# A hybrid attention block: priority of weight parts and of the differential heads' norms, a shared tile, and one more temporary

## The chip, the cores and the metric

The kernel runs on one core of a Trainium2 chip. The metric is the time of one execution on the device in microseconds; of several executions the median counts. A profile comes from one further execution, whose own time is named beside its span.

## The reference

One decoder block over 512 tokens of width 1024, in float32. Two attention branches share one input projection; a gated sum of both, an output projection, a residual and a feed-forward part follow.

```python
xn = rmsnorm(x, norm_mix_g)
proj = xn @ w_in          # q_lat, kv_lat, k_rope, dq, dk, dv, gate_pre
# branch A: 8 heads of latent attention, 64 + 32 rotated columns each
q = rmsnorm(q_lat) @ w_uq;  kv = rmsnorm(kv_lat) @ w_ukv
o_mla = causal_attention(cat(q_nope, rope(q_pe)), cat(k_nope, rope(k_rope)), v)
# branch B: 4 differential heads, each of two softmaxes over 64 columns
o_diff = rmsnorm(attn(dq1, dk1, dv) - lam * attn(dq2, dk2, dv), subln_g) * (1 - lambda_init)
gates = sigmoid(gate_pre + b_gate)
merged = g_mla * (o_mla @ w_branch_mla) + g_diff * (o_diff @ w_branch_diff)
x = x + merged @ w_out
x = x + (silu(hn @ w_ffn_gate) * (hn @ w_ffn_up)) @ w_ffn_down    # hn = rmsnorm(x)
return rmsnorm(x, norm_final_g)
```

## The kernel before

Every product is made of three: both operands are split into a high and a low part in the format that TensorE multiplies at speed (`split`, L242 to L252: ScalarE makes the high part at L245 or L247, VectorE the low part at L249 or L251), and `mm3` (L298 to L300) adds high x high, high x low and low x high in one PSUM tile. A matmul covers 128 rows, 128 of the contraction and up to 512 columns, the whole sequence.

A weight tile goes through `weights` (L267 to L294): SyncE's queue loads it into one of four `raw` buffers, then a high part (L260 on ScalarE) and a low part (L265 on VectorE) go to one of three `w` buffers. I call these two the weight parts.

Work is issued in program order with priorities, of which the lower number goes first, and a scheduler makes from them one fixed list per engine. Everything has the priority 1000000 and counts up, but for two blocks: `feed` starts at 1000, so it goes before all else, and `attention` at 100000, entered with `urgent()`, goes before the ordinary work (L126 to L141). Before the change the weight parts are in `feed` (L280), and so are a few steps of rotations and gates (L558, L480). Within its list an engine runs strictly in order: an instruction that waits holds up all behind it.

The stages, with their times in the profile: input norm and projections to the latents (to about 55 us), the eight heads of the latent attention in four pairs (to about 203 us), the four differential heads (to about 290 us), the branch products, then output projection and feed-forward. During the attention, `fill` issues matmuls that don't depend on the heads at hand: up-projections, rotations and gates of later heads (lists FILL, FILL_MLA, FILL_DIFF). They are what TensorE does while ScalarE and VectorE work on the softmax.

In the attention, `scores` (L617 to L635) makes the products of a block of 128 queries (L626), subtracts the masked maximum (L630), takes the exponential (L158 on ScalarE) and the reciprocal of the sum (L633). `transposed` (L644 to L656) transposes the probabilities (L652) and splits them into `PT` (L245, L249), and `values` (L658 to L667) multiplies by v (L663) into `ps_pv`. In the differential heads two such maps are subtracted (L678 to L680). Rotations (L554 to L561) are a shuffle (L557), a product with a table (L558), another product (L559) and a sum (L560), then a split; the rotated rows are then copied into the heads' tiles by DMAs from SyncE's queue (`L<-L` in the profile).

A differential head ends with copies of its output and its square (L686, L687 on ScalarE), the split of the square (L690 on VectorE, L691 on GpSimd) into a tile `sqs`, and its norm `diff_norm` (L694 to L708): two matmuls with ones sum the squares (L698), then come a logarithm and an exponential (L700, L701), four steps on VectorE and GpSimd (L702 to L705), and a split into a new tile `o` (L706). The main loop (L810 to L819) calls for head h: the first entry of the filling list, the norm of head h - 1 at ordinary priority, the rest of the list, and the head with urgent priority. The last norm is urgent. Then come the sigmoids (L822) and `branch` (L783), which needs the outputs of the norms.

PSUM has three buffers for `ps_mm`, two for `ps_sc`, two for `ps_tr` and one for `ps_pv`. Of the tiles of 512 columns there are 22 in two parts (`L`), five temporaries (`t`) and six of probabilities (`P`).

Of the kernel before, what the change touches and what calls it, by code (L numbers as in the profile page):

```python
# [2 lines left out]

# [1 line left out]

# [16 lines left out]
P = 128  # L22
# [13 lines left out]
OFF = (0, 512, 896, 1152)  # L36
MAGIC = 12582912.0
TWO_PI = 6.283185
BUFS = dict(X=2, L=22, P=6, PT=1, raw=4, w=3, t=5, sm=24)
LAST = 256  # L40
N_WARM = 10
P_DVE = (0, 1)
# [8 lines left out]
FILL_DIFF = [[("qk", 2), ("gate", 0, 3)],  # L51
             [("qk", 3), ("gate", 0, 4), ("gate", 0, 5)],
             [("gate", 0, 6), ("gate", 0, 7), ("gate", 1, 0)],
             [("gate", 1, m) for m in range(1, KD)]]
# [34 lines left out]
def build(ctx, nc, tc, a, out):  # L89
# [5 lines left out]
    def nm(s):  # L95
        uid[0] += 1
        return f"{s}_{uid[0]}"

    def T(tag, shape, dtype):
        return sb.tile(shape, dtype, name=nm(tag), tag=tag, bufs=BUFS[tag])  # L100

# [3 lines left out]
    def L_():  # L105
        return T("L", [P, 2, S], F32R)
# [13 lines left out]
    def dma(o, i):  # L120
        nc.sync.dma_start(out=o, in_=i)
# [14 lines left out]
            tc.cur_priority = self.saved  # L136

    attention, feed = Ahead(100000), Ahead(1000)

    def urgent():  # L140
        return attention  # L141
# [115 lines left out]
    def round_hi(o, i):  # L257
        if w_eng[0] == 'act':
            with tc.issue_after(hi_last.ins):
                nc.scalar.activation(out=o, in_=i, func=AF.Copy)  # L260
        else:
            nc.vector.tensor_copy(out=o, in_=i)

    def round_lo(o, i, hi):
        (nc.vector if w_eng[1] == 'dve' else nc.gpsimd).tensor_sub(out=o, in0=i, in1=r32(hi))  # L265

    def weights(src, n0, n1, pick=None):  # L267


        raw = T("raw", [P, 1024], F32)  # L270
        n = n0 * n1
        rv = raw[:, :n].rearrange("p (a b) -> p a b", a=n0)
        if isinstance(src, list):
            for i, s_ in enumerate(src):
                dma(rv[:, i, :].rearrange("p (h d) -> p h d", h=s_.shape[1]), s_)
        else:
            dma(rv, src)
        w = T("w", [P, 2, 1024], F32R)
        if pick is None:
            with feed:  # L280
                round_hi(w[:, 0, :n], raw[:, :n])
                round_lo(w[:, 1, :n], raw[:, :n], w[:, 0, :n])
        else:
            nk = sum(h * (d1 - d0) for h, d0, d1 in pick)
            wv = [w[:, s, :n0 * nk].rearrange("p (a b) -> p a b", a=n0) for s in range(2)]
            c = 0
            for h, d0, d1 in pick:
                src_ = rv.rearrange("p a (h e) -> p a h e", h=h)[:, :, :, d0:d1]
                hi, lo = [v[:, :, c:c + h * (d1 - d0)].rearrange("p a (h e) -> p a h e", h=h) for v in wv]
                c += h * (d1 - d0)  # L290
                round_hi(hi, src_)
                round_lo(lo, src_, hi)
            n = n0 * nk
        return [w[:, i, :n].rearrange("p (a b) -> p a b", a=n0) for i in range(2)]  # L294
# [198 lines left out]
    def fill(work):  # L493
        for kind, *args in work:
            if kind == "gate":
                gate(*args)
            elif kind == "v":
                diff_v(*args)
            elif kind == "qk":
                qk[args[0]] = diff_qk(*args)  # L500
            elif kind == "pe":
                pe[args[0]] = mla_pe(*args)
            elif kind == "mv":
                mv[args[0]] = mla_v(*args)
            elif kind == "mqk":
                mqk[args[0]] = mla_qk(*args)
            elif kind == "mr":
                mla_rope(args[0], mqk[args[0]], pe[args[0] // 2])
# [164 lines left out]
    def diff_head(h, products):  # L673
        blocks = []
        for i, p1 in enumerate(prob_tiles()):
            p2 = T("P", [P, S], F32)[:, :(i + 1) * P]
            r1, r2 = scores(list(zip(products, (p1, p2))), i)
            nc.vector.tensor_mul(out=r2, in0=r2, in1=neg_lam)  # L678
            nc.scalar.activation(out=p2, in_=p2, func=AF.Copy, scale=r2)
            nc.vector.scalar_tensor_tensor(out=p1, in0=p1, scalar=r1, in1=p2, op0=ALU.mult, op1=ALU.add)  # L680
            blocks.append(p1)
        pt = transposed(blocks)
        ps = values(pt, lambda j, s: dv[(h // 2) * 2 + j // 2][:, s, (j % 2) * 256 + (h % 2) * P:
                                                              (j % 2) * 256 + (h % 2) * P + P])
        o32, sq = tmp(), tmp()
        nc.scalar.activation(out=o32, in_=ps, func=AF.Copy)  # L686
        nc.scalar.activation(out=sq, in_=ps, func=AF.Square)  # L687
        sqs = L_()
        sqs = [sqs[:, 0, :], sqs[:, 1, :]]
        nc.vector.tensor_copy(out=sqs[0], in_=sq)  # L690
        nc.gpsimd.tensor_sub(out=sqs[1], in0=sq, in1=r32(sqs[0]))  # L691
        return o32, sqs

    def diff_norm(o32, sqs):  # L694

        ps = PS("tr")
        for s in range(2):
            nc.tensor.matmul(out=ps, lhsT=ones_r, rhs=sqs[s], start=s == 0, stop=s == 1)  # L698
        y, u = tmp(), tmp()
        log_exp(out=y, in_=ps, func=AF.Ln, scale=1.0 / P, bias=eps)  # L700
        last_exp[0] = log_exp(out=y, in_=y, func=AF.Exp, scale=-0.5)  # L701
        nc.vector.scalar_tensor_tensor(out=u, in0=ps, scalar=P * EPS, in1=y, op0=ALU.add, op1=ALU.mult)  # L702
        nc.vector.scalar_tensor_tensor(out=u, in0=u, scalar=-0.5 / P, in1=y, op0=ALU.mult, op1=ALU.mult)
        nc.gpsimd.tensor_mul(out=o32, in0=o32, in1=y)
        nc.vector.scalar_tensor_tensor(out=u, in0=u, scalar=1.5, in1=o32, op0=ALU.add, op1=ALU.mult)  # L705
        o = L_()  # L706
        split(u, o[:, 0, :], o[:, 1, :], col(R_SG))
        return o  # L708

# [27 lines left out]
    def mla_rope(p, qk, pe):  # L737
        for h, (q, k) in enumerate(qk):
            r0 = 32 * (2 * (p % 2) + h)
            dma(r32(q[64:96, :, :]), r32(pe[r0:r0 + 32, :, :]))  # L740
            dma(r32(k[64:96, :, :]), r32(kpe))
# [59 lines left out]
    for p in range(4):  # L801
        o = L_()
# [6 lines left out]

    o_diff, parts = [], []  # L810
    for h in range(4):
        fill(FILL_DIFF[h][:1])
        if h > 0:
            o_diff.append(diff_norm(*parts[h - 1]))
        fill(FILL_DIFF[h][1:])
        with urgent():
            parts.append(diff_head(h, qk[h]))
    with urgent():
        o_diff.append(diff_norm(*parts[3]))  # L819
# [19 lines left out]
    for c in range(8):  # L839
        half, kp = c // 4, c % 4  # L840
        raw = T("raw", [P, 1024], F32)
        dma(raw.rearrange("p (a b) -> p a b", a=2), kview("w_out", half * S, S, 2 * kp, 2))
        w = None
        if c < 3:
            w = T("w", [P, 2, 1024], F32R)
        elif c == 3:
            w = T("PT", [P, 2, 1280], F32R)
# [36 lines left out]
    for f, n in products[:3]:  # L884
        w = weights(kview(n, f * P, P), KD, P)
# [5 lines left out]
    for n_, (f, n) in enumerate(products):  # L891
        if n_ < 3:
            ps, w = early[n_]
            ffn_product(ps, w, 256, 512)
        else:
            w = weights(kview(n, f * P, P), KD, P)
# [50 lines left out]
    for half in range(2):  # L947
# [8 lines left out]
        for k0 in range(0, NF, 2):  # L956
            w = weights(kview("w_ffn_down", half * S, S, k0, 2), 2, S)
# [42 lines left out]
```

## Time and profile before

| what | value |
|---|---|
| runs | 749.06, 749.19, 750.64 us; median 749.19 |
| profiled execution | 749.08 us, span 747.3 us |
| mean granted clock of TensorE | 0.995 |
| matmuls (PE) | 731.1 us busy, 98% |
| weight loads (PEld) | 618.2 us, 83% |
| VectorE (DVE) | 416.9 us, 56% |
| ScalarE (ACT) | 332.5 us, 44% |
| GpSimd (POOL) | 49.9 us, 7% |

The span runs from the first to the last instruction that the profile counts. PE is TensorE's matmuls, PEld its loads of the stationary operand, SP SyncE, whose queue issues the DMAs. In rows of the trace an instruction is named by its line, its engine, its operation and its tiles (output, then inputs, without numbers); in brackets stands how long its engine had been idle, and whose result came last.

### The profile page before, as it was taken

How to read it: one execution, taken by the hardware profiler on the slowest of the kernel's cores; microseconds unless marked ns; L12 is line 12 of the kernel's file. 1: busy time of each engine (PE TensorE's matmuls, PEld its weight loads, DVE VectorE, ACT ScalarE, POOL GpSimd, SP SyncE). 2: the span in 40 equal slices, each digit the busy share in tenths (PEclk: the TensorE clock that was granted, in tenths of full speed). 3: DMA queues.
4: the chain of work that ended last, by engine and by line, in shares of the span. 5: the costliest groups of instructions: out<-in, count | busy, mean ns of one | idle time of the engine just before them, and what ended most of it. 6: DMA issues, size and time to landing. Idle time of an engine off the chain costs nothing.

```text
span 747.3 us, 9538 instructions
## 1 busy us (share of the span) xinstructions
PE 731.1 (98%) x3602; PEld 618.2 (83%) x3602; DVE 416.9 (56%) x812; ACT 332.5 (44%) x613; POOL 49.9 (7%) x45
## 2 busy tenths in 40 slices
PE   9998999999989989999999999999999999999996
PEld 7977999888868878888898888888888888888885
DVE  7787798988897765695544333342333332122424
ACT  7764788767665633643414232222323222122314
POOL 1000000321240101000000000000000000000302
PEclk9999999999999999999999999999999999999999
DMA  9615344523432312339114333323233232323202
GB/s 336 197 50 137 102 116 100 134 65 97 113 85 63 107 57 85 113 114 281 29 56 114 99 98 89 110 84 113 84 102 96 87 110 86 112 86 109 89 1 112
DMA packets 100414, 78.82 MB, mean 105 GB/s; under 512 B 6416, under 2 KB 87056, under 8 KB 100368
## 3 DMA queue, kind: packets, MB, share of 16 engines
q1 hardware_dynamic: 100080, 78.13, 35.5%
q8 instruction: 28, 0.46, 0.3%
q14 instruction: 18, 0.15, 0.1%
q10 hardware_dynamic: 288, 0.08, 0.0%
HBM read 71.91 MB, written 2.10 MB: 99 GB/s over the span
## 4 chain that ended last, share of the span: by engine, by line
PE 68%; DVE 6%; ACT 2%; issue 1%; DMA 0%; DVEq 0%; ACTq 0%
PE ps_mm L298 19%; PE ps_mm L299 19%; PE ps_mm L300 19%; DVE w L265 2%; PE ps_sc L298 1%; PE ps_sc L300 1%; PE ps_tr L300 1%; PE ps_tr L298 1%; PE ps_tr L299 1%; PE ps_sc L299 1%; DVE P L630 1%; PE ps_pv L300 1%; PE ps_pv L298 1%; PE ps_pv L299 1%; DVE L L249 1%
## 5 line engine op out<-in xcount | busy, mean ns | idle before, releaser
L265 DVE TENSOR_TENSOR w<-raw,w 128x1024 fp32r<-128x1024 f32 (+3 forms) x114 | 136.1, 1196 | 160.7 <-ACT w L260 160.0
L260 ACT ACTIVATE w<-raw 128x1024 fp32r<-128x1024 f32 (+3 forms) x110 | 109.5, 998 | 254.3 <-issue 154.6
L298 PE MATMUL ps_mm<-X,w 128*128 128x512 f32 (+1 forms) x568 | 217.8, 384 | 4.7 <-DVE t L558 4.6
L299 PE MATMUL ps_mm<-X,w 128*128 128x512 f32 (+1 forms) x568 | 217.7, 383 | 0.0
L300 PE MATMUL ps_mm<-X,w 128*128 128x512 f32 (+1 forms) x568 | 217.3, 383 | 0.0
L298 PEld LDWEIGHTS ps_mm<-X,w 128*128 128x128 f32 x568 | 107.1, 189 | 26.0 <-issue 2.8
L299 PEld LDWEIGHTS ps_mm<-X,w 128*128 128x128 f32 x568 | 107.3, 189 | 20.0 <-issue 0.2
L300 PEld LDWEIGHTS ps_mm<-X,w 128*128 128x128 f32 x568 | 107.2, 189 | 20.0
L905 DVE TENSOR_TENSOR t<-t,ps_mm 128x512 f32<-128x512 f32 x22 | 15.1, 688 | 66.4 <-PE ps_mm L300 65.7
L158 ACT ACTIVATE P<-P,sm 128x128 f32<-128x128 f32 (+3 forms) x64 | 35.7, 558 | 25.6 <-DVE sm L630 25.2
L931 POOL TENSOR_TENSOR L<-L,P 128x512 f32<-128x512 f32 (+1 forms) x9 | 12.6, 1414 | 436.2 <-ACT t L930 436.2
L626 PE MATMUL ps_sc<-L,L 96*128 96x128 f32 (+7 forms) x160 | 36.6, 324 | 1.2 <-DVE sm L630 1.2
L299 PE MATMUL ps_mm<-w,L 128*128 128x512 f32 (+1 forms) x100 | 37.2, 372 | 0.0
L298 PE MATMUL ps_mm<-w,L 128*128 128x512 f32 (+1 forms) x100 | 37.1, 373 | 0.0
L300 PE MATMUL ps_mm<-w,L 128*128 128x512 f32 (+1 forms) x100 | 37.0, 373 | 0.0
L299 PE MATMUL ps_mm<-L,w 128*128 128x512 f32 x90 | 35.4, 394 | 0.0
L298 PE MATMUL ps_mm<-L,w 128*128 128x512 f32 x90 | 35.2, 393 | 0.0
L300 PE MATMUL ps_mm<-L,w 128*128 128x512 f32 x90 | 35.2, 391 | 0.0
L245 ACT ACTIVATE L<-t 64x512 fp32r<-64x512 f32 (+2 forms) x47 | 29.2, 621 | 10.2 <-DVE t L779 3.7
L630 DVE CUSTOM_DVE_ANT_0 P<-ps_sc,mask 128x128 f32<-128x128 f32 (+3 forms) x64 | 30.6, 477 | 3.5 <-PE ps_sc L626 3.3
L626 PEld LDWEIGHTS ps_sc<-L,L 96*128 96x128 f32 (+1 forms) x160 | 27.1, 189 | 4.9 <-DVE sm L630 1.7
L249 DVE TENSOR_TENSOR L<-t,L 128x512 fp32r<-128x512 f32 (+2 forms) x37 | 27.7, 749 | 3.6 <-ACT L L245 3.1
(271 smaller groups left out, 1136.6 us busy)
## 6 DMA issues: line engine op xcount, KB each, us to landing
raw<-w_in SPq DMA_DIRECT2D x28, 512.0 KB, 4.5
raw<-w_ffn_gate SPq DMA_DIRECT2D x22, 512.0 KB, 3.9
raw<-w_ffn_up SPq DMA_DIRECT2D x22, 512.0 KB, 3.9
raw<-w_ffn_down SPq DMA_DIRECT2D x22, 512.0 KB, 3.6
L<-x SPq DMA_DIRECT2D x8, 512.0 KB, 7.4
L<-L SPq DMA_DIRECT2D x32, 128.0 KB, 3.4
raw<-w_out SPq DMA_DIRECT2D x8, 512.0 KB, 3.8
L<-xt SPq DMA_DIRECT2D x8, 256.0 KB, 4.3
```

The lines of the kernel that those rows point to most:

```text
L158: return nc.scalar.activation(**kw)
L245: nc.scalar.activation(out=hi, in_=src, func=AF.Copy, scale=scale)
L249: nc.vector.tensor_sub(out=lo, in0=src, in1=r32(hi))
L260: nc.scalar.activation(out=o, in_=i, func=AF.Copy)
L265: (nc.vector if w_eng[1] == 'dve' else nc.gpsimd).tensor_sub(out=o, in0=i, in1=r32(hi))
L298: nc.tensor.matmul(out=o, lhsT=lh, rhs=rh, start=start, stop=False)
L299: nc.tensor.matmul(out=o, lhsT=lh, rhs=rl, start=False, stop=False)
L300: return nc.tensor.matmul(out=o, lhsT=ll, rhs=rh, start=False, stop=stop)
L626: nc.tensor.matmul(out=ps[:, :n], lhsT=q[:, i * P:n], rhs=k[:, 0:n], start=j == 0, stop=j == last)
L630: nc.vector.tensor_tensor_reduce(out=m, in0=ps[:, :n], in1=mask[:, S - n:], scale=-1.0, scalar=3.4e38, op0=ALU.add, op1=ALU.min, accum_out ...
L905: nc.vector.tensor_mul(out=g, in0=g, in1=ps)
L931: nc.gpsimd.tensor_mul(out=xs, in0=xs, in1=g)
```

## The change

Four edits:

1. The weight parts lose their place ahead of all else up to the differential heads: a flag `parts_first`, set at the first of them, decides whether `weights` enters `feed`. Until then they have the ordinary priority of the place where they are issued.
2. `diff_norm` of head h - 1 moves behind the whole filling list of head h, and is urgent: it stands right ahead of `diff_head(h)`.
3. The norm's output goes into the tile of the squares, whose last reader is the sum; one `L` tile less is taken per head.
4. There are six temporaries `t` in place of five.

```diff
--- before.py
+++ after.py
@@ -1,5 +1,5 @@
 import math
-from contextlib import ExitStack
+from contextlib import ExitStack, nullcontext
 
 import numpy as np
 
@@ -36,7 +36,7 @@
 OFF = (0, 512, 896, 1152)
 MAGIC = 12582912.0
 TWO_PI = 6.283185
-BUFS = dict(X=2, L=22, P=6, PT=1, raw=4, w=3, t=5, sm=24)
+BUFS = dict(X=2, L=22, P=6, PT=1, raw=4, w=3, t=6, sm=24)
 LAST = 256
 N_WARM = 10
 P_DVE = (0, 1)
@@ -136,6 +136,7 @@
             tc.cur_priority = self.saved
 
     attention, feed = Ahead(100000), Ahead(1000)
+    parts_first = [False]
 
     def urgent():
         return attention
@@ -277,7 +278,7 @@
             dma(rv, src)
         w = T("w", [P, 2, 1024], F32R)
         if pick is None:
-            with feed:
+            with feed if parts_first[0] else nullcontext():
                 round_hi(w[:, 0, :n], raw[:, :n])
                 round_lo(w[:, 1, :n], raw[:, :n], w[:, 0, :n])
         else:
@@ -685,13 +686,13 @@
         o32, sq = tmp(), tmp()
         nc.scalar.activation(out=o32, in_=ps, func=AF.Copy)
         nc.scalar.activation(out=sq, in_=ps, func=AF.Square)
-        sqs = L_()
-        sqs = [sqs[:, 0, :], sqs[:, 1, :]]
+        o = L_()
+        sqs = [o[:, 0, :], o[:, 1, :]]
         nc.vector.tensor_copy(out=sqs[0], in_=sq)
         nc.gpsimd.tensor_sub(out=sqs[1], in0=sq, in1=r32(sqs[0]))
-        return o32, sqs
-
-    def diff_norm(o32, sqs):
+        return o32, sqs, o
+
+    def diff_norm(o32, sqs, o):
 
         ps = PS("tr")
         for s in range(2):
@@ -703,7 +704,6 @@
         nc.vector.scalar_tensor_tensor(out=u, in0=u, scalar=-0.5 / P, in1=y, op0=ALU.mult, op1=ALU.mult)
         nc.gpsimd.tensor_mul(out=o32, in0=o32, in1=y)
         nc.vector.scalar_tensor_tensor(out=u, in0=u, scalar=1.5, in1=o32, op0=ALU.add, op1=ALU.mult)
-        o = L_()
         split(u, o[:, 0, :], o[:, 1, :], col(R_SG))
         return o
 
@@ -809,11 +809,11 @@
 
     o_diff, parts = [], []
     for h in range(4):
-        fill(FILL_DIFF[h][:1])
-        if h > 0:
-            o_diff.append(diff_norm(*parts[h - 1]))
-        fill(FILL_DIFF[h][1:])
+        parts_first[0] = True
+        fill(FILL_DIFF[h])
         with urgent():
+            if h > 0:
+                o_diff.append(diff_norm(*parts[h - 1]))
             parts.append(diff_head(h, qk[h]))
     with urgent():
         o_diff.append(diff_norm(*parts[3]))
```

Both programs have the same instructions. Line numbers of the changed code are one higher from L139 of the old to the removed line in `diff_norm`. Their order differs from VectorE's row 125 and ScalarE's row 72 on, and up to about row 1556 of TensorE, ahead of the branch products.

The first place is VectorE ahead of the first rotations, at about 55 to 60 us. `ps_mm_686` is an up-projection, `ps_tr_716` and `ps_mm_737` are products that are rotated, and `w_762` holds the weights of the gate `ps_mm_765`, whose matmuls come next on TensorE. Before:

```order
L265 TENSOR_TENSOR w_762<-raw_760,w_762 128x1024
L251 SCALAR_TENSOR_TENSOR L_677<-ps_mm_686,L_677 64x512
L265 TENSOR_TENSOR w_794<-raw_792,w_794 128x512
L557 STREAM_SHUFFLE t_723<-ps_tr_716 32x512
L558 TENSOR_TENSOR t_722<-ps_tr_716,tab_605 32x512
L557 STREAM_SHUFFLE t_749<-ps_mm_737 128x512
L558 TENSOR_TENSOR t_748<-ps_mm_737,tab_605 128x512
L251 SCALAR_TENSOR_TENSOR L_678<-ps_mm_686,L_678 64x512
```

After:

```order
L252 SCALAR_TENSOR_TENSOR L_677<-ps_mm_686,L_677 64x512
L266 TENSOR_TENSOR w_762<-raw_760,w_762 128x1024
L252 SCALAR_TENSOR_TENSOR L_678<-ps_mm_686,L_678 64x512
L266 TENSOR_TENSOR w_794<-raw_792,w_794 128x512
L558 STREAM_SHUFFLE t_723<-ps_tr_716 32x512
L559 TENSOR_TENSOR t_722<-ps_tr_716,tab_605 32x512
L558 STREAM_SHUFFLE t_749<-ps_mm_737 128x512
L559 TENSOR_TENSOR t_748<-ps_mm_737,tab_605 128x512
```

The two splits that read `ps_mm_686` now stand ahead of the shuffles (L557 before, L558 after), with one weight part between them and one behind. On ScalarE the two high parts that go with them stand one place further forward each.

The second place is VectorE in the first differential head, at about 203 to 209 us. `t_2362` and `t_2363` belong to the rotation of the queries of head 3, `t_2409` and `t_2410` to that of its keys, `P_25..` are probabilities of head 1, `PT_2292` the transposes of head 0. Before:

```order
L249 TENSOR_TENSOR PT_2292<-ps_tr_2306,PT_2292 128x384
L630 ISA P_2564,sm_2572<-ps_sc_2566,mask 128x512
L630 ISA sm_2572 128x1
L265 TENSOR_TENSOR w_2675<-raw_2673,w_2675 128x1024
L680 SCALAR_TENSOR_TENSOR P_2541<-P_2541,sm_2551,P_2542 128x384
L633 RECIPROCAL sm_2574<-sm_2573 128x1
L557 STREAM_SHUFFLE t_2363<-ps_mm_2337 128x512
L558 TENSOR_TENSOR t_2362<-ps_mm_2337,tab_595 128x512
L557 STREAM_SHUFFLE t_2410<-ps_mm_2384 128x512
```

After:

```order
L266 TENSOR_TENSOR w_2660<-raw_2658,w_2660 128x1024
L250 TENSOR_TENSOR PT_2292<-ps_tr_2306,PT_2292 128x384
L634 RECIPROCAL sm_2550<-sm_2549 128x1
L631 ISA P_2541,sm_2554<-ps_sc_2543,mask 128x384
L631 ISA sm_2554 128x1
L558 STREAM_SHUFFLE t_2363<-ps_mm_2337 128x512
L559 TENSOR_TENSOR t_2362<-ps_mm_2337,tab_595 128x512
L558 STREAM_SHUFFLE t_2410<-ps_mm_2384 128x512
L559 TENSOR_TENSOR t_2409<-ps_mm_2384,tab_595 128x512
```

The rotation of the queries now follows the split of the transposes and one subtraction of a maximum (L631 after the change), and the keys' product (L559) follows its shuffle. The weight part `w_2675` is no longer between, another one, `w_2660`, stands ahead of the split.

The third place is TensorE at the norm of head 1. `ps_pv_2607` before and `ps_pv_2606` after are head 1's values, `ps_sc_31..` scores of head 3, `ps_mm_2709` a gate; the sum of squares is L698 before and L699 after. Before, the last values and what follows them:

```order
L663 MATMUL ps_pv_2607<-PT_2587,L_932 128x512
L663 MATMUL ps_pv_2607<-PT_2587,L_932 128x384
L663 MATMUL ps_pv_2607<-PT_2587,L_986 128x256
L663 MATMUL ps_pv_2607<-PT_2587,L_986 128x128
L626 MATMUL ps_sc_3103<-L_2370,L_2368 128x128
L626 MATMUL ps_sc_3103<-L_2370,L_2369 128x128
L299 MATMUL ps_mm_2709<-X_61,w_2706 128x512
L300 MATMUL ps_mm_2709<-X_61,w_2706 128x512
```

and, 12 rows of that gate further on, the sum:

```order
L298 MATMUL ps_mm_2709<-X_62,w_2706 128x512
L299 MATMUL ps_mm_2709<-X_62,w_2706 128x512
L300 MATMUL ps_mm_2709<-X_62,w_2706 128x512
L626 MATMUL ps_sc_3104<-L_2370,L_2368 128x128
L626 MATMUL ps_sc_3104<-L_2370,L_2369 128x128
L698 MATMUL ps_tr_2659<-L_2624,ones_r 128x512
```

After:

```order
L664 MATMUL ps_pv_2606<-PT_2586,L_932 128x512
L664 MATMUL ps_pv_2606<-PT_2586,L_932 128x384
L664 MATMUL ps_pv_2606<-PT_2586,L_986 128x256
L664 MATMUL ps_pv_2606<-PT_2586,L_986 128x128
L627 MATMUL ps_sc_2805<-L_2121,L_2120 128x512
L627 MATMUL ps_sc_3100<-L_2370,L_2368 128x128
L627 MATMUL ps_sc_3100<-L_2370,L_2369 128x128
L627 MATMUL ps_sc_3101<-L_2370,L_2368 128x128
L627 MATMUL ps_sc_3101<-L_2370,L_2369 128x128
L699 MATMUL ps_tr_2721<-L_2623,ones_r 128x512
```

Between the last values and the sum there were four scores and seventeen matmuls of the gate; now there are five scores.

## The prediction

> **What bounds the kernel now.** I read the page's first two parts, then PE's waits, then the timelines of PE, DVE and ACT round each of those waits. First the page: the span and the busy times.
>
> ```profile
> span 747.3 us, 9538 instructions
> PE 731.1 (98%) x3602; PEld 618.2 (83%) x3602; DVE 416.9 (56%) x812; ACT 332.5 (44%) x613; POOL 49.9 (7%) x45
> ```
>
> PE is busy for 98% of the span. The change alters no instruction, only the order, and as many matmuls take as long as before. So all that it can win is PE's idle time and time at a lower clock. PE's waits between 40 and 720 us, grouped by the waiting line and the one waited for, with total, number and longest:
>
> ```profile
> PE ps_mm L298 <- DVE t L558: 4.6, 2, 2.4
> PE ps_sc L626 <- DVE sm L630: 1.2, 1, 1.2
> PE ps_pv L663 <- DVE PT L249: 1.1, 1, 1.1
> PE ps_pv L663 <- ACT PT L245: 1.0, 2, 0.6
> PE ps_mm L298 <- DVE L L480: 0.2, 1, 0.2
> ```
>
> That is 8.1 us in all. Where they lie is in PE's timeline (start, duration, then in brackets idle time and releaser):
>
> ```profile
> 57.19 0.39 PE L299 MATMUL ps_mm<-L,w 128*128 128x512 f32 x1
> 57.42 0.40 PE L300 MATMUL ps_mm<-L,w 128*128 128x512 f32 x1
> 60.20 0.47 PE L298 MATMUL ps_mm<-X,w 128*128 128x512 f32 x1 [2.38 <-DVE t L558]
> 61.19 0.52 PE L299 MATMUL ps_mm<-X,w 128*128 128x512 f32 x1
> ...
> 64.83 0.39 PE L299 MATMUL ps_mm<-X,w 128*128 128x512 f32 x1
> ...
> 73.65 0.85 PE L626 MATMUL ps_sc<-L,L 96*128 96x128 f32 x6
> ...
> 208.69 0.50 PE L298 MATMUL ps_mm<-X,w 128*128 128x512 f32 x1 [2.21 <-DVE t L558]
> ...
> 224.34 0.72 PE L626 MATMUL ps_sc<-L,L 128*128 128x512 f32 x2 [1.21 <-DVE sm L630]
> ...
> 268.83 1.10 PE L663 MATMUL ps_pv<-PT,L 128*128 128x384 f32 x4 [0.63 <-ACT PT L245]
> ...
> 271.07 0.44 PE L663 MATMUL ps_pv<-PT,L 128*128 128x384 f32 x1 [1.14 <-DVE PT L249]
> ...
> 271.67 0.50 PE L298 MATMUL ps_mm<-X,w 128*128 128x512 f32 x1 [0.15 <-DVE L L480]
> ```
>
> Matmuls of 512 columns start 0.23 us apart (57.19, 57.42) and last 0.40, so a stall costs its idle time and 0.17 more. After the first stall comes a second loss: the nine steps from 61.19 to 64.83 take 3.64 us where nine times 0.23 is 2.05. It is a clock row in the table of windows (the columns are the stretch, its length, the busy times of PE, PEld, DVE, ACT and POOL, then the granted clock):
>
> ```profile
> 61.07:64.48 3.41, 3.41 (x10) 2.61 (x9) 3.38 (x7) 1.23 (x2) 0.00 (x0) 0.54 0.31 78
> 207.80:211.30 3.50, 2.61 (x11) 2.17 (x12) 3.50 (x11) 0.82 (x2) 3.09 (x3) 1.00 0.61 150
> 75.00:203.00 128.00, 128.00 (x765) 114.03 (x765) 112.77 (x285) 94.70 (x207) 17.84 (x12) 1.00 0.41 103
> 203.00:290.00 87.00, 81.28 (x388) 66.54 (x388) 63.22 (x139) 42.64 (x88) 15.79 (x11) 1.00 0.30 84
> ```
>
> So four places lose time: 57 to 65 us, 2.38 + 0.17 + 1.6 = 4.15; 206 us, 2.38; 222 us, 1.38; and 267 to 272 us, 0.63 + 1.14 + 0.15 with three times 0.17, 2.43. Together 10.3 us. Between 75 and 203 us PE never waits, though DVE is busy for 112.8 of 128 us.
>
> **The change at 57 us.** These are DVE's rows there.
>
> ```profile
> 55.16 1.23 DVE L265 TENSOR_TENSOR w<-raw,w 128x1024 fp32r<-128x1024 f32 x1 [0.20 <-ACT w L260]
> 56.30 0.68 DVE L251 SCALAR_TENSOR_TENSOR L<-ps_mm,L 64x512 fp32r<-64x512 f32 x1
> ...
> 59.38 0.66 DVE L558 TENSOR_TENSOR t<-ps_mm,tab 128x512 f32<-128x512 f32 x1
> 60.08 0.69 DVE L251 SCALAR_TENSOR_TENSOR L<-ps_mm,L 64x512 fp32r<-64x512 f32 x1
> ...
> 65.77 0.69 DVE L251 SCALAR_TENSOR_TENSOR L<-t,L 128x512 fp32r<-128x512 f32 x1
> 67.55 0.69 DVE L480 TENSOR_TENSOR L<-ps_mm,x_rms 128x512 f32<-128x512 f32 x1 [1.09 <-PE ps_mm L300]
> 68.16 0.41 DVE L265 TENSOR_TENSOR w<-raw,w 128x256 fp32r<-128x256 f32 x1
> ```
>
> The gate's first matmul (the start at 60.20) needs a free ps_mm buffer. Three go round, and before, both readers of the older product ps_mm_686 ended only at 60.08 + 0.69, behind the rotations, so the gate took the rotation's buffer at 60.04. In the new order the two L251 that read ps_mm_686 stand on either side of one weight part, and the rotations behind them. From 55.16 on, 0.6 + 1.15 + 0.65 gives 57.6: the gate's buffer is free just as PE gets there at 57.65. The stall and the half-clock stretch behind it go, and PE comes to the first scores 4.15 us earlier, at 69.5 instead of 73.65.
>
> But these scores need the rotated rows, which SP copies:
>
> ```profile
> L121 SPq DMA_DIRECT2D L<-L x8: 507/563/1834, 65.7 to 76.2; - x8
> DMA to landing us min/median/max: 2.3/3.9/4.8
> ```
>
> DVE does the same work as before up to the last L560, without a gap, so it is no earlier there. Behind it the new order has a weight part (0.35) and L480 (0.62), both free by then as the gate's matmuls end at 63.3, ahead of the two splits of rotated rows. The second split therefore ends at 66.46 + 0.97 = 67.4. With the median of 3.9 us to landing the copy is there at 71.3, and PE has stood since 69.6. About 1.8 us of the 4.15 come back as a new wait of the first scores: **net 2.3**, bounds 0 (copies landed at 73.5, by the maximum of 4.8 and one more copy ahead in the queue, 0.5 to 1.8) and 4.0 (2.3 us to landing). The raw load which SP now issues ahead of the copies waits for a weight part at about 64 and is out before they are ready, so I cost it at nothing; if not, it lies within the lower bound.
>
> **75 to 203 us.** The weight parts now stand behind attention steps, and attention steps further on in PE's order among the filling matmuls. No stall was there, and counting the matmuls ahead of each step in the new order at 0.23 us leaves every one some cover; I take nothing, bounds 0 and 1 lost.
>
> **At 206 us** PE waits for the rotation of q of head 3:
>
> ```profile
> 202.82 0.54 DVE L630 CUSTOM_DVE_ANT_0 P<-ps_sc,mask 128x384 f32<-128x384 f32 x1
> ...
> 204.14 0.16 DVE L633 RECIPROCAL sm<-sm 128x1 f32<-128x1 f32 x1 [0.77 <-ACT P L158]
> ...
> 204.52 0.56 DVE L249 TENSOR_TENSOR PT<-ps_tr,PT 128x384 fp32r<-128x384 f32 x1
> ...
> 207.35 0.72 DVE L557 STREAM_SHUFFLE t<-ps_mm 128x512 f32<-128x512 f32 x1
> ```
>
> From the copy of the transposes to the rotation are 207.35 - 204.52 = 2.83 us. In the new order only a reciprocal and one L630 of 384 stand between: 0.47 + 0.1 + 0.5 = 1.1, so 1.7 sooner. A weight part of 1.15 now stands ahead of the copy, and 0.77 of it fits in the gap at 204.14, so 0.4 is given back: **1.3 to 1.4**, I take 1.4 (bounds 0 and the whole 2.38). The sixth temporary lets the rotation of k follow at once.
>
> **At 222 and 267 us** the new order puts filling matmuls between the steps that follow closely before. Head 1's scores get two blocks of the gate between them, and the values of head 3 some 5 us of matmuls behind their transposes where 0.3 was. DVE is busy for 63.2 of the 87 us from 203 on, so it has room. Both stalls go: **1.4 and 2.4** (bounds: half of each, all).
>
> **The norms.** Those of heads 0, 2 and 3 have 4.9 us and more of matmuls between the last values and the sum. For head 1 only five scores stand there: one of 512 columns (0.23) and four of 128, which I put at 0.11 each: two take 0.39 in the row at 234.22 below, run-out of 0.17 included. That is 0.7. What must happen meanwhile is in the rows of before:
>
> ```profile
> 233.41 0.97 PE L663 MATMUL ps_pv<-PT,L 128*128 128x256 f32 x6
> 234.22 0.39 PE L626 MATMUL ps_sc<-L,L 128*128 128x128 f32 x2
> ...
> 234.42 0.60 ACT L686 ACTIVATE t<-ps_pv 128x512 f32<-128x512 f32 x1 [1.90 <-PE ps_pv L663]
> ...
> 235.53 0.43 DVE L690 CAST L<-t 128x512 fp32r<-128x512 f32 x1 [1.15 <-ACT t L687]
> ```
>
> The values end at 234.38 and the cast at 235.96, 1.6 us later; the sum of squares starts 0.1 behind that. So PE waits 1.0 us and loses **1.2** (bounds 0.3, where a missing record misled me on the cover, and 2.4, where a weight part of 1.15 stands ahead of the cast on DVE). The tile shared by squares and output only spares a buffer, and the norm's output is first needed in the branch stage; nothing for both.
>
> **The sum.** 2.3 + 1.4 + 1.4 + 2.4 - 1.2 = 6.3 us. The profiled execution took 749.08, its span of 747.3 and 1.8 around it, and stands 0.11 below the median of the three runs, so 749.08 - 6.3 = **742.8**.
>
> **Rivals.**
>
> The first stall is only swapped: the copies land at 73.5, and the first scores start where they started. For it speaks that DVE is no earlier. It leaves 1.4 + 1.4 + 2.4 - 1.2 = 4.0: 745.1. Chance 0.15.
>
> A new stretch at half clock: after an idle time of 2.38 us the clock fell to 0.54 for 3.41 us, after one of 2.21 us (207.80 to 211.30) it stayed at 1.00. The waits that I expect are 1.8, 1.0 and 1.0 us; should one grow by half a microsecond, 1.6 us more go: 744.4. Chance 0.10. The Trainium skill (TensorE: Matmul & The Clock Gate, the closing table's advice against drops in mid-kernel) sets the limit at idle gaps over about 3 us, one window; by it this rival couldn't happen and its chance would go to the forecast. The trace's 2.38 us gap with its clock row speaks against that limit.
>
> What is won is lost again before the feed-forward: the last norm's sums come later among the branch matmuls, which need its output. If that wait takes 5 us, about one norm's chain on DVE, ACT and POOL, 748 to 749 remains. Against it: they still have a head start by my count. Chance 0.10.
>
> Slower: DVE becomes the bound between 75 and 203 us. The 20 weight parts there no longer go first, and a weight part behind an attention step that itself waits for PE or ACT holds up the filling matmuls. These are the 20 parts (busy time, mean ns, then idle time before them):
>
> ```profile
> L265 DVE TENSOR_TENSOR w<-raw,w 128x1024 fp32r<-128x1024 f32 (+3 forms) x20 | 23.7, 1184 | 0.9 <-ACT w L260 0.5
> ```
>
> If each of the 20 comes 0.45 us too late, 9 us go, and 742.8 + 9 = 751.8. It decides from 0.4 us a part on (8 us, more than the sum and 1.5). For it: 88% of DVE is taken. Against: three weight buffers run ahead of PE. Chance 0.07.
>
> **How the numbers follow.** The forecast has 0.56, the rivals 0.15, 0.10, 0.10 and 0.07; 0.02 is for gains beyond all bounds. About 0.2%, 1.5 us, is what a measurement of this kernel can tell from no change. Faster by more, under 747.7: 0.56 + 0.15 + 0.10 + 0.02 = 0.83, of which 0.02 may be lost by several lower bounds at once: 0.81. Within: 0.10 + 0.02 = 0.12. Slower: 0.07. The range reaches down to 740.6 (early part at 4.0, head 1's norm at 0.7) and up to 747.5, past both milder rivals: 745.1, 1.9 for half of the gains at 222 and 267 us, and 0.5 for half the bound between 75 and 203. It leaves out the last two rivals and little more.
>
> **What would show it.** Right: the gate's first matmul starts at about 57.7 without a wait and no clock row under 0.9 follows by 65; the first scores start at about 71.4 and wait for a DMA; a wait of about 1 us near 200 us for L559 (L558 before); no waits in the scores of head 1 and the values of head 3; a wait of about 1 us for L691 ahead of a sum of L699 (the changed code's numbers are one higher there). Wrong: waits on L266 between 75 and 203 us, first scores at 73 or later, a wait in the branch stage, or a second clock row at half.

## The result, and the profile after

The changed kernel takes **744.11 us**, the median of six runs (743.54 to 746.21), against 749.16 for the kernel before in the same stretch of time. The ratio is 0.9932, with a 95% interval of 0.9916 to 0.9948: 5.05 us less, between 3.9 and 6.3. The forecast was 742.8 us, with a range of 740.6 to 747.5.

PE's waits in the changed kernel between 40 and 740 us (line waiting, line waited for, total, number, longest), from a profiled execution that itself took 746.21 us, the longest of the six:

```profile
PE ps_sc L627 <- DVE sm L631: 2.0, 3, 0.9
PE ps_mm L299 <- DVE t L559: 0.8, 1, 0.8
PE ps_pv L664 <- ACT PT L246: 0.6, 1, 0.6
PE ps_sc L627 <- DMA L<-L: 0.6, 1, 0.6
```

That is 4.0 us where 8.1 were. Where they lie, in PE's timeline of the same profile:

```profile
57.19 0.40 PE L301 MATMUL ps_mm<-L,w 128*128 128x512 f32 x1
57.52 0.47 PE L299 MATMUL ps_mm<-X,w 128*128 128x512 f32 x1
...
70.33 0.93 PE L627 MATMUL ps_sc<-L,L 96*128 96x128 f32 x6 [0.63 <-DMA L<-L]
...
187.44 0.50 PE L299 MATMUL ps_mm<-X,w 128*128 128x512 f32 x1 [0.75 <-DVE t L559]
...
200.09 0.62 PE L627 MATMUL ps_sc<-L,L 128*128 128x384 f32 x2 [0.34 <-DVE sm L631]
201.34 0.83 PE L664 MATMUL ps_pv<-PT,L 128*128 128x512 f32 x2 [0.64 <-ACT PT L246]
...
203.40 1.22 PE L627 MATMUL ps_sc<-L,L 128*128 128x512 f32 x2 [0.78 <-DVE sm L631]
...
238.06 0.44 PE L627 MATMUL ps_sc<-L,L 128*128 128x128 f32 x2 [0.88 <-DVE sm L631]
```

The four old places are gone: the gate starts at 57.52 without a wait, the scores of head 1 and the values of head 3 no longer wait, and the wait of 2.21 us for a rotation has broken up. In their place stand one at the first scores, one at 187, three at 200 to 203 and one at 238 us. With 0.17 us added to each, as in the prediction, the old places cost 10.3 us, of which 1.6 are the stretch at half clock behind the first of them, and the new ones 4.0 + 6 x 0.17 = 5.0 without their clock.

The profiled execution lost more, though, at half clock. In the windows (stretch, length, busy times of PE, PEld, DVE, ACT and POOL, granted clock) the changed kernel shows:

```profile
199.00:204.40 5.40, 3.64 (x13) 2.19 (x12) 4.43 (x14) 4.00 (x9) 0.00 (x0) 0.87 0.40 97
204.40:209.80 5.40, 5.40 (x18) 4.60 (x17) 5.40 (x16) 2.61 (x6) 3.52 (x3) 0.50 0.38 97
```

No idle time there is longer than 0.78 us, yet the clock stands at 0.50 for 5.4 us. By their mean granted clock, 0.995 to 0.997 against this one's 0.994, four of the other five executions had less of this or none; they took 743.5 to 744.3. The fifth stands at 0.994 and took 745.3.

### The profile page after: what moved, and what is told of

Read it like the earlier page. It is cut to its first block, busy times and chain, and to the rows that moved or that the text cites. A ratio compares the mean times of both kernels' runs of the same rounds, so it can differ in the third digit from the quotient of the medians.

```text
span 744.4 us, 9551 instructions
## 1 busy us (share of the span) xinstructions
PE 732.0 (98%) x3602; PEld 619.1 (83%) x3602; DVE 414.1 (56%) x812; ACT 333.6 (45%) x613; POOL 49.9 (7%) x45
## 4 chain that ended last, share of the span: by engine, by line
PE 93%; DVE 4%; DMA 1%; ACT 1%; issue 1%; DVEq 0%; ACTq 0%; SPq 0%
PE ps_mm L300 24%; PE ps_mm L301 24%; PE ps_mm L299 24%; PE ps_sc L627 3%; PE ps_tr L653 2%; PE ps_tr L301 2%; PE ps_sc L299 2%; PE ps_tr L299 2%; PE ps_sc L300 2%; PE ps_sc L301 2%; PE ps_tr L300 2%; PE ps_pv L774 1%; PE ps_pv L664 1%; DVE w L266 1%; PE ps_pv L301 1%; PE ps_pv L300 1%
## 5 line engine op out<-in xcount | busy, mean ns | idle before, releaser
L266 DVE TENSOR_TENSOR w<-raw,w 128x1024 fp32r<-128x1024 f32 (+3 forms) x114 | 133.9, 1177 | 160.9 <-ACT w L261 160.2
L627 PE MATMUL ps_sc<-L,L 96*128 96x128 f32 (+7 forms) x160 | 38.8, 336 | 2.6 <-DVE sm L631 2.0
L631 DVE CUSTOM_DVE_ANT_0 P<-ps_sc,mask 128x128 f32<-128x128 f32 (+3 forms) x64 | 30.5, 477 | 8.1 <-PE ps_sc L627 7.4
```

What stands on the lines that cost most here:

```text
L627: nc.tensor.matmul(out=ps[:, :n], lhsT=q[:, i * P:n], rhs=k[:, 0:n], start=j == 0, stop=j == last)
L631: nc.vector.tensor_tensor_reduce(out=m, in0=ps[:, :n], in1=mask[:, S - n:], scale=-1.0, scalar=3.4e38, op0=ALU.add, op1=ALU.min, accum_out ...
```

## The experiments

All times are medians, in us; each ratio is against runs of the kernel before on the same chip. "Lowest" is the fastest single run. For the kernel before, the fastest runs are also those with the highest mean clock; for some of the others they are not (see the last section).

| what is done | median | lowest | ratio, 95% interval |
|---|---|---|---|
| kernel before (17 runs beside the second group) | 749.06 | 747.25 | |
| the change | 744.11 | 743.54 | 0.9932 (0.9916 to 0.9948) |
| weight parts ordinary up to the first list | 745.91 | 744.27 | 0.9954 (0.9941 to 0.9966) |
| two splits first, nothing else | 744.26 | 744.08 | 0.9931 (0.9918 to 0.9943) |
| weight parts ordinary in the eight heads alone | 750.68 | 749.04 | 1.0012 (1.0001 to 1.0023) |
| edit of the weight parts, whole | 747.59 | 746.71 | 0.9973 (0.9964 to 0.9982) |
| norms and shared tile | 744.37 | 742.93 | 0.9924 (0.9912 to 0.9937) |
| sixth temporary | 747.54 | 745.92 | 0.9962 (0.9949 to 0.9975) |
| norms, shared tile, temporary | 744.59 | 742.73 | 0.9938 (0.9922 to 0.9953) |
| the change without the temporary | 743.41 | 742.84 | 0.9922 (0.9907 to 0.9938) |
| the change without the shared tile | 743.62 | 743.41 | 0.9927 (0.9912 to 0.9942) |
| the change without the flag's reset | 743.85 | 743.39 | 0.9928 (0.9912 to 0.9945) |
| the change, weight parts ordinary up to the first list only | 740.33 | 740.30 | 0.9884 (0.9871 to 0.9897) |
| two splits first, norms, tile, temporary | 740.37 | 740.15 | 0.9883 (0.9864 to 0.9902) |

**Weight parts ordinary up to the first list.**

```diff
-            with feed:
+            with feed if parts_first[0] else nullcontext():
...
     fill(FILL[0])
+    parts_first[0] = True
     o_mla = []
```

> Weight parts at ordinary priority only up to the end of the first filling list, then ahead of all else as before; norms, tiles and temporaries as before. The order equals the changed kernel's up to the first scores, and the kernel before's kind of order behind them. Theory (the stall at 57 us and the half clock behind it are worth what the first scores gain, 3.2 us in the two profiles): 746.0 us, first scores at about 70.3, the waits at 206, 222 and 267 us still there. Rival (the half clock comes back elsewhere or the gain is lost behind the first scores): 748 to 749.

Measured 745.91, the theory's number. The first scores start at 70.27, as it had it. Behind 200 us it had not: where the kernel before waits six times, 5.7 us in all, this one waits seven times, 4.6 us in all, at other places (the wait of 2.21 us at 206 is one of 0.66), and its profile has a stretch at half clock at 224 us that the kernel before has not. That the number fits is in part chance.

**The edit of the weight parts alone, in full.**

```diff
-            with feed:
+            with feed if parts_first[0] else nullcontext():
...
     for h in range(4):
+        parts_first[0] = True
         fill(FILL_DIFF[h][:1])
```

> The edit of the weight parts alone, in full: ordinary priority up to the differential heads. The order equals the changed kernel's up to the middle of the first differential head. Theory 1 (this edit makes the whole gain, the later waits at 222 and 267 us go because attention steps stand further on among the filling matmuls): 744.1 us, as the changed kernel, with waits near 187 and 200 us. Theory 2 (the waits at 222 and 267 us go through the norms and the temporary): 744.1 + 1.4 + 2.4 = 747.9 us with both waits in the profile.

Measured 747.59: theory 2. PE still waits at 267 us, in this experiment's timeline:

```profile
266.87 1.10 PE L664 MATMUL ps_pv<-PT,L 128*128 128x384 f32 x4 [0.63 <-ACT PT L246]
268.82 1.56 PE L664 MATMUL ps_pv<-PT,L 128*128 128x384 f32 x7 [0.85 <-DVE PT L250]
```

The one at 222 us is gone here as well, so theory 2 holds for one of the two places. And the whole edit gains less than its early part alone: 1.6 against 3.3 us.

**Norms, tile and temporary alone.** This is the change without its two edits of `weights` and of the flag.

```diff
-        fill(FILL_DIFF[h][:1])
-        if h > 0:
-            o_diff.append(diff_norm(*parts[h - 1]))
-        fill(FILL_DIFF[h][1:])
+        fill(FILL_DIFF[h])
         with urgent():
+            if h > 0:
+                o_diff.append(diff_norm(*parts[h - 1]))
```

> Norms urgent, shared tile and sixth temporary alone; weight parts ahead of all else throughout, as before. Same order as the kernel before up to 206 us. Theory 1 (all from the weight parts): 749.2 us, no difference, or up to 1 us slower by a wait at the norm of head 1. Theory 2 (the waits at 222 and 267 us go through these edits): 749.2 - 3.8 + 1.0 = 746.4 us.

Measured 744.59: theory 2, and 1.8 us better than it. Neither of the two waits is left, and none at the norm of head 1.

**The change with only the early part of the weights' edit.**

```diff
     fill(FILL[0])
+    parts_first[0] = True
     o_mla = []
...
-        parts_first[0] = True
         fill(FILL_DIFF[h])
```

> The changed kernel, but weight parts ahead of all else again from the end of the first filling list on, not only from the differential heads on. Theory (the waits near 187 and 200 to 204 us and the stretch at 0.66 of the clock behind them come from weight parts that no longer go first in the eight heads): these go, the early gain stays: 749.2 - 3.2 = 746.0 with the wait at 206 us (2.4) back, less what the norms' edits save. If theory 2 of the later waits holds as well, 743.4. Rival (the order of the eight heads matters little): 744.1, as the changed kernel.

Measured 740.33, 3.8 us less than the change itself and below every number that was put down for it. The expectation had the wait at 206 us back in full; as in the first experiment, 0.66 us of it is left. The gains of that experiment and of norms, tile and temporary alone, 3.3 and 4.6 us by the medians, would make 741.3. What PE still waits for between 40 and 740 us is 1.7 us:

```profile
PE ps_tr L653 <- DVE t L703: 0.7, 1, 0.7
PE ps_mm L299 <- DVE t L559: 0.7, 1, 0.7
PE ps_pv L664 <- DVE PT L250: 0.3, 1, 0.3
```

**Two splits first.** The weight parts stay ahead of all else.

```diff
         for h in range(2):
-            split(ps[64 * h:64 * h + 64, :], q[h][0:64, 0, :], q[h][0:64, 1, :], MLA_SCALE)
+            with feed if p == 0 else nullcontext():
+                split(ps[64 * h:64 * h + 64, :], q[h][0:64, 0, :], q[h][0:64, 1, :], MLA_SCALE)
```

> The kernel before, with the weight parts where they were, but with the two splits of the first up-projection (ps_mm_686) ahead of all else. VectorE's rows round the first rotations are then those of the changed kernel. Theory (the stall at 57 us is the PSUM buffer that these two splits release; where the weight parts stand matters only through them): 745.9 us, as the run with only the early weight parts at ordinary priority, and no wait near 57 us. Rival (the weight parts themselves must come later, the buffer is not the cause): 749.2, the wait of 2.4 us still there.

Measured 744.26, and no wait near 57 us:

```profile
57.29 0.40 PE L300 MATMUL ps_mm<-L,w 128*128 128x512 f32 x1
57.60 0.47 PE L298 MATMUL ps_mm<-X,w 128*128 128x512 f32 x1
```

So it is enough to move these two splits, and by PE's row at 60.20 in the kernel before, whose wait ends with a reader of a ps_mm product, what they give back is the buffer. The scheduler makes from this edit the very lists that it makes from weight parts at ordinary priority up to the first list: the two programs agree row for row on all five engines. The early weight parts' own place thus has no effect beside the splits' place. As the programs are one, they make a comparison that wasn't planned. One program took 745.91 in one group and 744.26 in the other, and the windows of the two profiles show a stretch of the clock that makes most of it; first the one of 745.91 (profiled run 746.54), then the one of 744.26:

```profile
219.00:223.80 4.80, 2.90 (x13) 1.65 (x12) 4.80 (x15) 3.16 (x8) 1.34 (x1) 1.00 0.41 109
223.80:227.20 3.40, 3.40 (x10) 2.62 (x9) 3.40 (x10) 1.52 (x5) 0.00 (x0) 0.51 0.11 23
```

```profile
219.00:223.80 4.80, 2.96 (x13) 2.01 (x14) 4.80 (x16) 3.77 (x9) 0.81 (x1) 1.00 0.46 109
223.80:227.20 3.40, 3.40 (x17) 2.81 (x16) 3.38 (x8) 0.90 (x4) 0.00 (x0) 1.00 0.31 67
```

The same waits precede (PE busy for 2.90 and 2.96 of 4.80 us); in one run the clock falls to half for 3.4 us, in the other it doesn't. The mean clock of most other runs goes with it, 0.996 in the group of 745.91 and 0.998 or more in that of 744.26. The lowest runs of both, 744.27 and 744.08, agree.

**Weight parts ordinary in the eight heads alone.** As the first experiment, with the flag the other way round: True up to the end of the first list, False for the eight heads, True from the differential heads on.

> Weight parts at ordinary priority during the eight heads of the latent attention alone; ahead of all else before and behind. Theory (there the edit of the weight parts costs what the full edit loses against the early one, 747.6 - 745.9 = 1.7 us, by waits near 187 and 200 us): 750.9 us. Rival (the loss needs the early gain, since the attention then runs further ahead): 749.2, no difference.

Measured 750.68, the theory's size; the ratio's interval of 1.0001 to 1.0023 only just excludes no difference, but the lowest runs, 749.04 and 747.25, differ as much, and its profiled run, of 749.09 us, has no stretch at half clock. PE waits where the changed kernel does:

```profile
188.91 0.50 PE L299 MATMUL ps_mm<-X,w 128*128 128x512 f32 x1 [0.52 <-DVE t L559]
201.55 0.62 PE L627 MATMUL ps_sc<-L,L 128*128 128x384 f32 x2 [0.35 <-DVE sm L631]
202.81 0.83 PE L664 MATMUL ps_pv<-PT,L 128*128 128x512 f32 x2 [0.64 <-ACT PT L246]
204.87 0.73 PE L627 MATMUL ps_sc<-L,L 128*128 128x512 f32 x2 [0.78 <-DVE sm L631]
```

The wait at 57 us is there as before, and those at 267 us in part (0.63 and 0.85). Of the old wait at 206 us 0.16 us is left; at 222 to 225 us three waits of 0.24, 0.68 and 0.25 us stand in place of one of 1.21.

**Norms and shared tile without the temporary.** As the third experiment, with `t=5`.

> Norms urgent and shared tile, five temporaries, weight parts as before. Theory (the norms' place makes the 4.6 us that these edits and the temporary made together, the waits at 222 and 267 us and the stretch at half clock behind them): 744.6 us. Rival (it needs the sixth temporary, so that the rotations don't wait for the norms' tiles): 747 to 749.

Measured 744.37, as with the temporary. Only the old waits at 57 and 206 us are left, the second with the 0.4 us ahead of it:

```profile
PE ps_mm L298 <- DVE t L558: 4.6, 2, 2.4
PE ps_pv L663 <- ACT PT L245: 0.4, 1, 0.4
```

**The sixth temporary alone.**

```diff
-BUFS = dict(X=2, L=22, P=6, PT=1, raw=4, w=3, t=5, sm=24)
+BUFS = dict(X=2, L=22, P=6, PT=1, raw=4, w=3, t=6, sm=24)
```

> The sixth temporary alone. Theory (it only lets rotations and norms that are there run closer): 749.2 us, no difference beyond 1 us. Rival (the temporary is what frees the waits at 222 and 267 us): 744.6 to 746.

Measured 747.54, between theory and rival: it saves 1.5 us by another order in the differential heads. The saving lies at 267 us, where of 0.63, 1.14 and 0.15 us one wait of 0.64 is left; at 222 us, waits of 0.44 and 1.18 us stand in place of the one of 1.21.

**The change without the temporary.**

```diff
-BUFS = dict(X=2, L=22, P=6, PT=1, raw=4, w=3, t=6, sm=24)
+BUFS = dict(X=2, L=22, P=6, PT=1, raw=4, w=3, t=5, sm=24)
```

> The changed kernel with five temporaries. Alone the sixth gave 1.5 us (747.5 against 749.1), with the norms nothing that could be told (744.6 with, 744.4 without). Theory (norms and temporary save the same waits at 222 and 267 us, so with the norms moved the temporary is idle): 744.1 us, as the changed kernel. Rival (the temporary adds its 1.5 us here): 745.6.

Measured 743.41: the theory. With the norms moved, the temporary saves nothing. In this profile the wait of 0.88 us at 238 us is missing, and the lowest run, 742.84, lies 0.7 us under that of the change: if the sixth temporary does anything here, it costs.

**The change without the shared tile.**

```diff
-        o = L_()
-        sqs = [o[:, 0, :], o[:, 1, :]]
+        sqs = L_()
+        sqs = [sqs[:, 0, :], sqs[:, 1, :]]
...
+        o = L_()
         split(u, o[:, 0, :], o[:, 1, :], col(R_SG))
```

> The changed kernel with a tile of its own for the norm's output. TensorE's order is word for word that of the changed kernel, VectorE's differs in some seven rows after the heads. Theory (the shared tile only spares a buffer that nothing waits for): 744.1 us. Rival (without it the last norm's output waits for a buffer and the branch products for it): over 745.

Measured 743.62: the theory. Its profile, of a run of 743.41 us, has the waits of the changed kernel from 187 us on, with two more of 0.24 and 0.17 us at 204 and 206 us, and shows nearly that kernel without the fall of the clock:

```profile
199.00:204.40 5.40, 3.58 (x16) 2.21 (x16) 4.43 (x13) 4.00 (x9) 0.00 (x0) 1.00 0.37 97
204.40:209.80 5.40, 5.23 (x25) 4.09 (x24) 5.40 (x15) 2.84 (x7) 4.44 (x4) 1.00 0.37 97
```

**The change without the flag's reset.**

```diff
     for h in range(4):
-        parts_first[0] = True
         fill(FILL_DIFF[h])
```

> The changed kernel without the flag being set at the differential heads: weight parts at ordinary priority there too, and behind them. TensorE's order is word for word that of the changed kernel; on VectorE one weight part changes places with a sum of probabilities at the end of the eight heads. Theory (what the flag restores from the differential heads on carries next to nothing): 744.1 us, within 1 us. Rival (weight parts behind the attention steps hold up the gates there): 745.5 or more.

Measured 743.85: the theory. That the weight parts go first again from the differential heads on carries nothing that these runs can tell.

**Two splits first, with norms, tile and temporary.** The changed kernel without its edit of `weights` and flag, and with the two splits in `feed` as above.

> Weight parts ahead of all else throughout as before; the first up-projection's two splits ahead of all else, norms urgent, shared tile, six temporaries. Theory (the whole gain is the freed PSUM buffer at 57 us and the norms; the weight parts' own place in the eight heads only costs): 740.3 us, as the run in which the weight parts are ordinary up to the first filling list. Rival (early weight parts at ordinary priority bring something of their own): 742 or more.

Measured 740.37: the theory. This program, too, agrees row for row with the one of 740.33 us, so the two are one measurement made twice. It beats both kernels: 8.8 us less than before, 3.7 less than the change.

## Why the prediction came out as it did

The time came out right, 1.3 us above the forecast, and its sign is what the waits said: PE was the bound, and its waits became fewer. The terms were less good than their sum. By the two profiles they are 3.2 at 57 us, -3.2 between 75 and 203, 2.4 at 206, 3.8 at 222 and 267, and -1.05 at head 1's norm, 5.1 in all; forecast were 2.3, 0, 1.4, 3.8 and -1.2. That the term left at nothing didn't break the sum is luck: two others were 0.9 and 1.0 too small. The 1.6 us at half clock behind the first stall are in the first term; the stretch at half clock that the changed kernel's profile shows comes on top.

**The stall at 57 us.** Right in its mechanism, and shown: moving the two splits that free the buffer takes it away. The second split of ps_mm_686 ended at 57.37 (forecast 57.6). These are its row and that of the last split of rotated rows in VectorE's timeline of the changed kernel, and then the landing of the copies to the heads' tiles between 60 and 80 us:

```profile
56.68 0.69 DVE L252 SCALAR_TENSOR_TENSOR L<-ps_mm,L 64x512 fp32r<-64x512 f32 x1
...
66.29 0.67 DVE L252 SCALAR_TENSOR_TENSOR L<-t,L 128x512 fp32r<-128x512 f32 x1
```

```profile
DMA to landing us min/median/max: 2.4/3.0/3.4
```

The term was too small: 2.3 forecast, 3.2 in the profiles. The first scores came at 70.33, not 71.3, since the second split ended at 66.96 (67.4 forecast) and the copies landed in 3.0 us (3.9 taken, the median of before). That 3.9 was one execution's: in the four other profiles in which the gate still waits, the median of these copies is 2.8 to 3.4 us, in the nine with an early gate 2.3 to 3.0. The 3.2 are 73.65 - 70.33, less the 0.23 by which the matmul ahead of the gate already stood earlier (57.42 and 57.19), and 0.12 for a matmul of 256 columns that now goes ahead of the scores. In five of the nine profiles with an early gate the scores didn't wait at all.

**75 to 203 us.** The step that failed. I took nothing, with 1 us as the bound. PE loses 0.75 + 0.17 at 187 and 0.34 + 0.64 + 0.78 + 3 x 0.17 at 200 to 203 us, 3.2 in all. The experiment with weight parts ordinary in these heads alone makes these waits and 1.6 to 1.8 us, since nearly all of the old wait at 206 us goes at the same time. The rival that a weight part behind an attention step holds up PE named this edit and this stage, but not what happened: PE waits for no weight part (L266) there, and the price was nowhere near 9 us. VectorE's rows show what PE waits for instead:

```profile
185.46 0.69 DVE L631 CUSTOM_DVE_ANT_0 P<-ps_sc,mask 128x512 f32<-128x512 f32 x1 [1.55 <-PE ps_sc L627]
...
186.72 0.67 DVE L559 TENSOR_TENSOR t<-ps_mm,tab 128x512 f32<-128x512 f32 x1
...
198.15 1.22 DVE L266 TENSOR_TENSOR w<-raw,w 128x1024 fp32r<-128x1024 f32 x1
...
199.62 0.40 DVE L631 CUSTOM_DVE_ANT_0 P<-ps_sc,mask 128x256 f32<-128x256 f32 x1
```

At 185 us a rotation for which PE waits stands behind an L631 that itself waited 1.55 us for its scores. At 198 us a weight part of 1.1 us stands ahead of the L631 whose result PE wants at 200.09. That the new order of these heads makes the waits is shown by the runs with and without it; that each goes back to the row named here is read from the list, not tested. My count had set each step against the filling matmuls ahead of it, and not against what its own engine was made to wait for.

**206 us.** The wait of 2.21 us did go, 2.38 with its run-out against 1.4 forecast, but the three waits at 200 to 203, counted above, cost 2.27 of that again. From the split of the transposes to the rotation are 205.41 - 204.40 = 1.0 us, as priced. But the split itself comes at 204.40, where it came at 204.52 before, though PE stood 3.2 us earlier at the first scores: what was won there is spent at 187 and 200 to 203 us. The wait of about 1 us for L559 near 200 us that was to be seen didn't come; the one for L559 is at 187. In the run without the shared tile, at full clock there, waits of 0.24 and 0.17 us are left at 204 and 206 us; in this profile the half clock may hide them.

**222 and 267 us.** Right in size: none of the 1.4 + 2.4 is left. The text put it down to the new order as a whole. By the runs the norms' place, with the shared tile, does it alone. It is not the only thing that can: the weight parts alone take away the wait at 222 us and leave those at 267, and the sixth temporary alone takes away most of those at 267.

**The norm of head 1.** Right in size, not in form: 0.88 + 0.17 against 1.2. PE doesn't wait for the cast but for the L631 ahead of the last scores, which stands behind a weight part that itself waited 1.52 us for its high part, and the cast behind it:

```profile
236.17 1.23 DVE L266 TENSOR_TENSOR w<-raw,w 128x1024 fp32r<-128x1024 f32 x1 [1.52 <-ACT w L261]
237.31 0.68 DVE L631 CUSTOM_DVE_ANT_0 P<-ps_sc,mask 128x512 f32<-128x512 f32 x1
...
237.92 0.42 DVE L691 CAST L<-t 128x512 fp32r<-128x512 f32 x1
```

This was the case behind the upper bound of that term.

**The rivals.** The swapped stall didn't come. No wait came in the branch stage. The new stretch at half clock did, in the profiled execution and by the clock in some others, though no wait had grown to 2.4 us as I asked for. That condition was wrong: I had read a limit between 2.21 and 2.38 us out of two rows of one profile, and other profiles have both gaps with the other outcome (last section).

The parts don't quite add up. By the lowest runs the whole edit of the weight parts gives 746.71 - 747.25 = -0.5 and the rest 742.73 - 747.25 = -4.5, together -5.0, where the change has 743.54 - 747.25 = -3.7. Together they order the differential heads in a way that neither has alone, the wait of 0.88 us at 238 us among it; what else of that order costs the 1.3 us was not separated. Without the sixth temporary that wait is absent and the rest is smaller: -0.5 and, for norms and shared tile, 742.93 - 747.25 = -4.3, against 742.84 - 747.25 = -4.4.

## What to carry to other kernels

Look in a stall of the bound engine for the buffer it waits for, and for the last reader of the product that holds it: two splits moved by one line gave here all that the ordinary priority of the early weight parts gave, without what it costs in the eight heads. A change of priority should end where its reason ends: kept up to the first list it is worth 3.3 us by the medians (3.1 by the lowest runs), kept through eight heads it gives 1.7 of that back (2.4 by the lowest runs). In an in-order list, count for each moved step what stands ahead of it and waits, not only what stands ahead of it and works.

## What the runs showed of the hardware

The clock can fall to half without a long gap, and does so in some executions of one and the same program. Before the change it fell after a gap of 2.38 us; after it, behind a stretch in which PE was busy for 3.64 of 5.40 us with no gap over 0.78; and in one program it fell once and not another time behind the same waits. Nor does a gap of one length always do it. The first row is the stretch behind the gap of 2.38 us at 57 us in the run with weight parts ordinary in the eight heads alone; the second that behind the gap of 2.21 us at 206 us in the run with norms, tile and temporary:

```profile
61.07:64.48 3.41, 3.41 (x17) 2.82 (x16) 3.38 (x7) 1.23 (x2) 0.00 (x0) 1.00 0.30 66
207.80:211.30 3.50, 2.53 (x6) 2.05 (x7) 3.31 (x8) 0.71 (x2) 3.01 (x3) 0.58 0.56 150
```

In the kernel before, the same two rows have 0.54 and 1.00. Advice that counts only gaps of about 3 us, such as the Trainium skill's on the page TensorE: Matmul & The Clock Gate, in the section Why this matters for your kernels, doesn't cover this, and the measurement decides. The Trainium skill's other statement on that page, under The HAM clock gate in its Part 1, that the window runs freely against the kernel, agrees with it.

A stretch of 3.4 us at half clock costs about 1.6 us where PE is the bound, and the runs of the kernel before fall into steps of that size. Of the 17 runs of the kernel before beside the second group, two took 747.25 and 747.37 (granted clock 0.998), nine 748.8 to 749.2 (0.995 to 0.996), and six 750.4 to 750.8 (0.994). A median of five runs therefore carries an accident of about 1.6 us: the same program gave 745.91 and 744.26. Differences of that size were told here by the lowest runs and by the rows of the clock.

Not all of the spread is the clock's. The whole edit of the weight parts took 746.71 us in its fastest run, whose profile stands at half clock from 202 to 209 us, while runs of it with a mean clock of 0.999 took 746.84 to 747.85:

```profile
202.00:209.00 7.00, 6.52 (x19) 5.55 (x20) 6.57 (x17) 3.66 (x10) 3.63 (x3) 0.51 0.29 75
```

What else differs between these executions no profile here shows, so the lowest run is not always the one with the fewest such stretches, and the readings above that rest on lowest runs alone are the less certain for it.
